# Hybrid decoder trunk on one core: the order of the first loads, and the place of the step that lays the tokens' norm factors along rows

## The chip, the cores and the metric

The kernel runs on one core of one Trainium2 chip. The metric is device time in microseconds (us) of one execution, as the median of several. The engines are named as in the profile: PE (matrix multiplies), PEld (its weight loads), DVE, ACT, POOL, and SP, whose only work here is to issue DMAs. Times inside the program are us from the start of the profiled span.

## The reference, cut to what matters

Two layers over 512 tokens of width 1024, in float32. Each layer normalizes the tokens, projects them with one large matrix, runs two kinds of attention over eight and four heads, gates, projects back and adds; then it adds a gated embedding.

```python
def rmsnorm(x, g, eps=RMS_EPS):
    xf = x.astype(jnp.float32)
    y = xf * lax.rsqrt(jnp.mean(xf * xf, axis=-1, keepdims=True) + eps)
    return (y * g.astype(jnp.float32)).astype(x.dtype)
...
    u = rmsnorm(h, norm_gain) @ w_in
    qa, ka, va, ga, qd, kd, vd, gd = jnp.split(u, list(np.cumsum(IN_SPLITS)[:-1]), axis=-1)
...
    y = jnp.concatenate([oa * jax.nn.silu(ga), od * jax.nn.silu(gd)], axis=-1) @ w_out
    h = h + y
    gate = jax.nn.sigmoid(rmsnorm(h, ple_norm_gain) @ w_ple_gate)
    return h + (p_i @ w_ple) * gate
```

Of `rmsnorm` the gain `g` belongs to a channel and the factor `rsqrt(mean(x*x)+eps)` to a token. The kernel uses that: it multiplies the gain into `x` ahead of the matmul and the token's factor into the result behind it.

## The kernel before, in words

**Precision and units.** A float32 operand is held as a high part and a low part (`hi`, `lo`), both in a rounded type; a product is three matmuls, high by high, high by low and low by high (`PASSES`, L317). A *unit* is one 128 x 512 result over 1024 channels: 8 blocks of 128 channels by 3, 24 matmuls with 512 columns. A *chunk* is four units, with a weight of 1024 x 512 that comes in four *pairs* (two blocks of channels, 512 KB each).

**Loads.** Every weight pair is loaded by SP into a staging tile (`stg`; three of them, and part of `of` as a fourth for the first chunk). ACT copies it into the ring (`ring`, five slots) as the high part, and DVE or POOL subtract to get the low part. The first layer's input comes twice: `xt`, the transpose (channels in rows), in four pieces of 512 KB, from which ACT makes the high parts (`xt_hi`: `xy<-fr,gt`, scaled by the gain) and DVE the low parts (`xt_lo`); and `x` by tokens, in four pieces of 512 KB, of which only the sums of squares are wanted (`x_sumsq` on ACT and DVE, then `rstd`: a tiny DVE step and a power on POOL for each of four groups of tokens, `st<-st`). `gt` holds the gains of the norms, 128 rows of 128 bytes. The first four pairs and `xt` pieces are needed together: pair r with piece r.

**The first chunk** (`vd`, `units_by_rows`, L482) goes by pairs, not by results: for pair r it does 6 matmuls into each of four results (banks `b_79` to `b_82`), 24 in all, and then takes pair r+1. Ahead of it PE runs `NWARM` matmuls on a tile of zeros (`warm_up`, `b<-pt`), which need no load.

**spread** (L527). The projections of q and k come out with tokens along columns, so the factors are needed along rows. `spread` lets PE transpose the four columns of factors, each broadcast to 128 columns (`b<-idt,st`, four small matmuls); ACT copies the result (`cr<-b`), and DVE multiplies it into the two tables of rotation (`cr<-ct,b`). Its first use is the rotation of the first q of the second chunk; the gates use it later. Its call for the first layer is L647, with a place of 2.5, in units of the plan (a chunk spans 4).

**What sets the order.** Nothing is written out in the order in which it runs. `Plan` gives each step a place; `Machine.schedule` (L189) takes all recorded instructions, gives each a wanted time (`want`: matmuls are laid end to end from `START`, everything else is counted back from its users, for a DMA by the lag in `lag`), and then plays the program against a table of costs: at each step it takes the engine that is free first and, of the instructions ready on it, the one with the earliest wanted time. The result is a fixed order on each engine. On the chip every engine takes its instructions in that order, so one that waits holds all behind it. SP's DMAs go through one queue; the model charges them at 230 bytes per ns (L272).

```python
            if e == "SP":
                t = max([t] + landed[-8:-7])
                free[e] = t + busy[i]
                dma = max(dma, t + 1.4) + done[i][1] / 230e3
```

The numbers of the cost model (L237, L272, `START`), `NWARM` and the place of `spread` are what the change touches.

Of the kernel before, what the change touches and what calls it, by code (L numbers as in the profile page):

```python
# [57 lines left out]
class Plan:  # L58
# [7 lines left out]
    def pe(self, t, us, f, *a):  # L66
        self.pieces.append((t, len(self.pieces), us, f, a))

    def at(self, t, us, f, *a):
        self.items.append((t, us, f, a))  # L70
# [16 lines left out]
class Machine:  # L87
# [101 lines left out]
    def schedule(self):  # L189
# [13 lines left out]
        busy, done = [0.0] * N, [None] * N  # L203
# [25 lines left out]

        clock, want = START, [None] * N  # L230
        for i in range(N):
# [4 lines left out]

        def lag(i):  # L237
            c = done[i]
            return c[0] + 2.0 + c[1] / 200e3 if isinstance(c, tuple) else c
        for i in range(N - 1, -1, -1):  # L240
            w = want[i] if want[i] is not None else end
            for s in succ[i]:
                w = min(w, want[s] - lag(i) - (MARGIN if eng[s] == "PE" and eng[i] != "PE" else 0.0))
            want[i] = w
# [4 lines left out]
        dma, landed = 0.0, []  # L249
# [5 lines left out]
        for _ in range(N):  # L255
            best = None
            for e, lst in waiting.items():
                if not lst:
                    continue
                t = max(free[e], min(ready_at[i] for i in lst))  # L260
                if best is None or t < best[0]:
                    best = (t, e)
            t, e = best
            i = min((i for i in waiting[e] if ready_at[i] <= t + 1e-9), key=lambda i: (want[i], i))
            waiting[e].remove(i)
            order.append((t, len(order), i))
            free[e] = t + busy[i]
            if e == "SP":

                t = max([t] + landed[-8:-7])  # L270
                free[e] = t + busy[i]
                dma = max(dma, t + 1.4) + done[i][1] / 230e3  # L272
                fin = dma + 0.6
                landed.append(fin)
            else:
                fin = t + done[i]
            for s in succ[i]:
                if eng[s] == "PE":

                    r = t + busy[i] if e == "PE" else fin + MARGIN  # L280
                else:
                    r = fin
                ready_at[s] = max(ready_at[s], r)
                left[s] -= 1
                if not left[s]:
                    waiting[eng[s]].append(s)
# [17 lines left out]

START = 8.0

MARGIN = 1.5

# [11 lines left out]
def trunk(tc, x, p, w_in, w_out, w_gate, w_ple, final_gain, tables, xt, gt, lams, sub, out):  # L322
# [7 lines left out]
    with tc.tile_pool(name="sb", bufs=1) as sb, tc.tile_pool(name="ps", bufs=1, space=PSUM) as psp, \  # L330
# [26 lines left out]
        RS0 = ST[:, 136:140]  # L357
# [38 lines left out]
        plan = Plan()  # L396
        at, pe = plan.at, plan.pe
        nbank = [0]
        NWARM = 14

        def bank():
            nbank[0] += 1
            return BANK[2 + (nbank[0] - 1) % 6]
# [123 lines left out]
        def spread(tt, rs, rot):  # L527
            b = {}

            def tr():  # L530
                b[0] = bank()
                for t in range(T):
                    PE.transpose(b[0][:, t * 128:(t + 1) * 128], rs[:, t:t + 1].to_broadcast([128, 128]), IDT)

            def f():
                ACT.activation(RB, b[0], AF.Copy)
                if rot:
                    DVE.tensor_mul(C0, C, b[0])
                    DVE.tensor_mul(SN0, SN, b[0])
            pe(tt, 0.436, tr)  # L540
            at(tt, 0.1, f)
# [57 lines left out]
        def warm_up():  # L599
            b = bank()  # L600
            for i in range(NWARM):
                mm(b, PT[:, 0, 0:128], PT[:, 0, 0:512], start=(i == 0), stop=(i == NWARM - 1))

# [23 lines left out]
        def st(us, f, *a):  # L627
            at(-10, 60 + us, f, *a)
# [13 lines left out]
        for t in range(T):  # L642
# [1 line left out]
            for h in range(2):  # L644
                st(3.1 + 0.3 * t, x_sumsq, t, h)
            st(3.2 + 0.3 * t, rstd, t, RS0)
        spread(2.5, RS0, True)  # L647


        nP = [0]  # L650
# [536 lines left out]
```

## Time and profile before

| what | value |
|---|---|
| median of three runs | 688.07 us (687.35 to 689.34) |
| profiled execution: its time | 687.14 us |
| profiled execution: its span | 685.1 us |
| PE busy | 672.7 us, 98% of the span |
| DVE, ACT, POOL busy | 435.1, 373.5, 383.4 us |
| chain that ended last | PE 94%, DVE 3%, DMA 1% |
| the DMAs from 12 to 24 us | some 410 GB/s |

The span runs from the first instruction to the last; 2.0 us of the profiled time lie outside it. A PE that is busy for 98% of the span leaves some 12 us in which it is not, and the timeline of PE shows where these are.

### The profile page before, as it was taken

How to read it: one execution, taken by the hardware profiler on the slowest of the kernel's cores; microseconds unless marked ns; L12 is line 12 of the kernel's file. 1: busy time of each engine (PE TensorE's matmuls, PEld its weight loads, DVE VectorE, ACT ScalarE, POOL GpSimd, SP SyncE). 2: the span in 40 equal slices, each digit the busy share in tenths (PEclk: the TensorE clock that was granted, in tenths of full speed). 3: DMA queues.
4: the chain of work that ended last, by engine and by line, in shares of the span. 5: the costliest groups of instructions: out<-in, count | busy, mean ns of one | idle time of the engine just before them, and what ended most of it. 6: DMA issues, size and time to landing. Idle time of an engine off the chain costs nothing.

```text
span 685.1 us, 9574 instructions
## 1 busy us (share of the span) xinstructions
PE 672.7 (98%) x3310; PEld 563.7 (82%) x3310; DVE 435.1 (64%) x839; ACT 373.5 (55%) x782; POOL 383.4 (56%) x290
## 2 busy tenths in 40 slices
PE   8999999999999999999999999999999999999995
PEld 6788888888888888888888888888888888788884
DVE  5447996657766884446443689874777678534334
ACT  6525756548888545524433457664787865353321
POOL 4669470876713357937484767266753245496311
PEclk9999999999999999999999999999999999999998
DMA  8656441444442532334152463333535262243002
GB/s 334 235 153 178 102 140 45 135 113 128 121 122 93 184 123 93 131 117 144 59 174 84 123 171 122 78 99 88 154 93 154 85 224 92 94 152 122 1 32 93
DMA packets 30961, 85.32 MB, mean 125 GB/s; under 512 B 4544, under 2 KB 4544, under 8 KB 30912
## 3 DMA queue, kind: packets, MB, share of 16 engines
q1 hardware_dynamic: 30912, 84.71, 39.9%
q8 instruction: 26, 0.43, 0.2%
q14 instruction: 23, 0.19, 0.1%
HBM read 63.72 MB, written 4.19 MB: 99 GB/s over the span
## 4 chain that ended last, share of the span: by engine, by line
PE 94%; DVE 3%; DMA 1%; issue 0%; ACT 0%; POOL 0%; SPq 0%; POOLq 0%; DVEq 0%; ACTq 0%
PE b L293 94%; DVE fr L293 2%; DMA gt<-in_gt_dram 1%; DVE misc L293 1%; DVE xy L293 0%; DVE ring L293 0%; POOL st L293 0%; ACT xy L293 0%; DVE of L293 0%; SPq L293 0%; DVE st L293 0%; POOLq L1183 0%; ACT of L293 0%; ACT misc L293 0%; DVEq L1183 0%
## 5 line engine op out<-in xcount | busy, mean ns | idle before, releaser
L293 PE MATMUL b<-xy,ring 128*128 128x512 f32 x1728 | 419.0, 393 | 0.2
L293 PEld LDWEIGHTS b<-xy,ring 128*128 128x128 f32 x1728 | 318.6, 188 | 63.6 <-DVE fr L293 1.9
L293 POOL TENSOR_TENSOR ring<-stg,ring 128x512 fp32r<-128x512 f32 x164 | 233.6, 1448 | 163.1 <-ACT ring L293 132.3
L293 PE MATMUL b<-ring,xy 128*128 128x512 f32 (+1 forms) x600 | 141.6, 385 | 2.6 <-ACT xy L293 2.4
L293 ACT ACTIVATE ring<-stg 128x1024 fp32r<-128x1024 f32 x95 | 99.9, 1057 | 51.4 <-PE b L293 33.5
L293 PEld LDWEIGHTS b<-ring,xy 128*128 128x128 f32 x600 | 107.4, 188 | 24.6 <-ACT xy L293 3.1
L293 ACT ACTIVATE fr<-fr,st 128x512 f32<-128x512 f32 (+3 forms) x193 | 101.7, 556 | 36.8 <-DVE st L293 34.2
L293 POOL TENSOR_TENSOR fr<-fr 128x512 f32<-128x512 f32 x53 | 74.0, 1399 | 30.1 <-ACT fr L293 25.6
L293 POOL TENSOR_TENSOR fr<-fr,cr 128x512 f32<-128x512 f32 x32 | 43.3, 1352 | 63.4 <-DVE fr L293 63.4
L293 DVE CUSTOM_DVE_ANT_0 fr<-b,ct 128x512 f32<-128x512 f32 (+3 forms) x128 | 58.5, 485 | 31.5 <-PE b L293 30.4
L293 DVE SCALAR_TENSOR_TENSOR xy<-fr,gt,xy 128x512 fp32r<-128x512 f32 x32 | 36.3, 1145 | 31.8 <-ACT xy L293 31.8
L293 PE MATMUL b<-qk 128*128 128x128 f32 (+3 forms) x256 | 52.4, 324 | 0.0
L293 DVE TENSOR_TENSOR ring<-stg,ring 128x512 fp32r<-128x512 f32 x26 | 34.7, 1334 | 21.7 <-ACT ring L293 21.7
L293 DVE TENSOR_TENSOR pt<-b,pt 128x384 fp32r<-128x384 f32 (+1 forms) x72 | 40.2, 592 | 12.0 <-ACT pt L293 11.6
L293 ACT ACTIVATE pt<-b 128x384 fp32r<-128x384 f32 (+1 forms) x72 | 34.6, 525 | 18.3 <-PE b L293 18.1
L293 PEld LDWEIGHTS b<-qk 128*128 128x128 f32 x256 | 39.0, 189 | 4.2 <-issue 0.3
L293 PEld LDWEIGHTS b<-idt,fr 128*128 128x128 f32 x284 | 34.0, 140 | 7.2 <-DVE fr L293 0.8
L293 ACT ACTIVATE nt<-fr 128x512 fp32r<-128x512 f32 x32 | 19.8, 624 | 36.7 <-POOL fr L293 36.7
L293 PE MATMUL b<-idt,fr 128*128 128x128 f32 x284 | 39.7, 272 | 0.0
L293 DVE TENSOR_TENSOR fr<-b,cr 128x512 f32<-128x512 f32 x48 | 32.6, 680 | 10.5 <-PE b L293 10.3
L293 POOL TENSOR_TENSOR st<-st 128x4 f32<-128x4 f32 (+1 forms) x20 | 18.0, 899 | 33.0 <-DVE st L293 32.4
L293 ACT ACTIVATE fr<-fr 128x512 f32<-128x512 f32 x26 | 16.4, 631 | 34.6 <-DVE fr L293 34.1
(78 smaller groups left out, 581.9 us busy)
## 6 DMA issues: line engine op xcount, KB each, us to landing
stg<-in_w_in_dram SPq DMA_DIRECT2D x63, 512.0 KB, 3.4
qk<-nt SPq DMA_DIRECT2D x128, 128.0 KB, 2.3
stg<-in_w_out_dram SPq DMA_DIRECT2D x16, 512.0 KB, 4.4
stg<-in_w_ple_gate_dram SPq DMA_DIRECT2D x16, 512.0 KB, 3.3
fr<-in_xt_dram SPq DMA_DIRECT2D x8, 512.0 KB, 5.3
stg<-in_w_ple_dram SPq DMA_DIRECT2D x4, 512.0 KB, 3.3
hsave<-fr SPq DMA_DIRECT2D x8, 256.0 KB, 2.0
fr<-hsave SPq DMA_DIRECT2D x4, 512.0 KB, 3.7
```

The lines of the kernel that those rows point to most:

```text
L293: getattr(self.eng[e], op)(*args, **kw)
```

## The change

In the cost model, a DMA of at most 64 KB is to be issued 4 us earlier than before with respect to its users, DMAs are charged at 300 instead of 230 bytes per ns, and the matmuls are laid out from 6.0 instead of 8.0 us. The warm-up has 10 matmuls instead of 14, and the first layer's `spread` has the place 3.3 instead of 2.5 (the first chunk spans 0 to 4). What is computed is the same.

```diff
         def lag(i):
             c = done[i]
-            return c[0] + 2.0 + c[1] / 200e3 if isinstance(c, tuple) else c
+            if isinstance(c, tuple):
+
+                return c[0] + (2.0 if c[1] > 65536 else 6.0) + c[1] / 200e3
+            return c
...
                 t = max([t] + landed[-8:-7])
                 free[e] = t + busy[i]
-                dma = max(dma, t + 1.4) + done[i][1] / 230e3
+                dma = max(dma, t + 1.4) + done[i][1] / 300e3
...
-START = 8.0
+START = 6.0
...
-        NWARM = 14
+        NWARM = 10
...
             for h in range(2):
                 st(3.1 + 0.3 * t, x_sumsq, t, h)
             st(3.2 + 0.3 * t, rstd, t, RS0)
-        spread(2.5, RS0, True)
+        spread(3.3, RS0, True)
```

Rows of the order below are one instruction each, or as many like it in a row as the `x` at the end says; the first word is a line of the kernel, and the changed kernel's lines are three further on (L296 for L293).

On SP, from the first DMA on, before:

```order
L293 DMA stg<-in_w_in_dram 128x1024
L293 DMA fr<-in_xt_dram 128x1024
L293 DMA gt<-in_gt_dram 128x32
L293 DMA stg<-in_w_in_dram 128x1024
L293 DMA fr<-in_xt_dram 128x1024
L293 DMA stg<-in_w_in_dram 128x1024
L293 DMA fr<-in_xt_dram 128x1024
L293 DMA fr<-in_x_dram 128x1024 x2
L293 DMA of<-in_x_dram 128x1024 x2
L293 DMA of<-in_w_in_dram 128x1024
L293 DMA fr<-in_xt_dram 128x1024
L293 DMA stg<-in_w_in_dram 128x1024 x3
```

And in the changed kernel:

```order
L296 DMA gt<-in_gt_dram 128x32
L296 DMA stg<-in_w_in_dram 128x1024
L296 DMA fr<-in_xt_dram 128x1024
L296 DMA stg<-in_w_in_dram 128x1024
L296 DMA fr<-in_xt_dram 128x1024
L296 DMA stg<-in_w_in_dram 128x1024
L296 DMA fr<-in_xt_dram 128x1024
L296 DMA of<-in_w_in_dram 128x1024
L296 DMA fr<-in_xt_dram 128x1024
L296 DMA fr<-in_x_dram 128x1024 x2
L296 DMA of<-in_x_dram 128x1024
L296 DMA stg<-in_w_in_dram 128x1024
```

The gains come first instead of third, the fourth weight pair and `xt` piece stand ahead of all of `x`, and the last piece of `x` now follows the first weight pair of the second chunk.

On ACT, in the first chunk, from the third `xt` piece to the end of the fourth, before (`cr<-b` is the copy of `spread`, `fr,st<-fr` and `of,st<-of` are sums of squares):

```order
L293 ACTIVATE xy_63<-fr,gt 128x512 x2
L293 ACTIVATE fr,st<-fr 128x512 x2
L293 ACTIVATE of,st<-of 128x512 x2
L293 ACTIVATE ring<-of 128x1024
L293 ACTIVATE cr<-b_86 128x512
L293 ACTIVATE xy_63<-fr,gt 128x512 x2
L293 ACTIVATE ring<-stg 128x1024 x2
```

And now, as far as the copy of `spread` (`xy_64<-b_79` to `xy_64<-b_81` write out results of the first chunk):

```order
L296 ACTIVATE xy_63<-fr,gt 128x512 x2
L296 ACTIVATE ring<-of 128x1024
L296 ACTIVATE xy_63<-fr,gt 128x512 x2
L296 ACTIVATE fr,st<-fr 128x512 x2
L296 ACTIVATE of,st<-of 128x512
L296 ACTIVATE ring<-stg 128x1024
L296 ACTIVATE of,st<-of 128x512
L296 ACTIVATE ring<-stg 128x1024
L296 ACTIVATE xy_64<-b_79,st 128x4x128
L296 ACTIVATE xy_64<-b_80,st 128x4x128
L296 ACTIVATE ring<-stg 128x1024
L296 ACTIVATE xy_64<-b_81,st 128x4x128
```

The high parts of the fourth `xt` piece stood behind `cr<-b`; now `cr<-b` comes only after three results are written out. On PE the four transposes of `spread` move in the same way, from ahead of the 24 matmuls of the fourth pair to behind the 18th of them.

Nor is the rest of the program in the same order. On PE 705 rows become 712, and in the attention parts of both layers groups of matmuls trade places. The first such place with transposes of attention weights (`b<-idt,fr`), before:

```order
L293 MATMUL b_79<-xy_63,ring 128x512 x9
L293 MATMUL b_86<-idt,fr 128x128 x3
L293 MATMUL b_81<-qk 128x128 x2
L293 MATMUL b_81<-qk 128x256 x2
L293 MATMUL b_82<-qk 128x384 x2
L293 MATMUL b_83<-qk 128x512 x2
L293 MATMUL b_84<-idt,fr 128x128 x4
L293 MATMUL b_85<-idt,fr 128x128 x3
L293 MATMUL b_79<-xy_63,ring 128x512 x6
```

And now:

```order
L296 MATMUL b_79<-xy_63,ring 128x512 x3
L296 MATMUL b_81<-qk 128x128 x2
L296 MATMUL b_81<-qk 128x256 x2
L296 MATMUL b_82<-qk 128x384 x2
L296 MATMUL b_83<-qk 128x512 x2
L296 MATMUL b_79<-xy_63,ring 128x512 x3
L296 MATMUL b_84<-idt,fr 128x128 x4
L296 MATMUL b_85<-idt,fr 128x128 x3
L296 MATMUL b_79<-xy_63,ring 128x512 x3
L296 MATMUL b_86<-idt,fr 128x128 x3
```

Here the scores `b<-qk` moved ahead by six matmuls of the projection and one group of transposes went to the end. The tail of the program, from the last chunk's last result on, is unchanged.

## Rows read from the trace of the kernel before

**Rows 1.** The page: busy time, share and count of each engine.

```profile
PE 672.7 (98%) x3310; PEld 563.7 (82%) x3310; DVE 435.1 (64%) x839; ACT 373.5 (55%) x782; POOL 383.4 (56%) x290
```

**Rows 2.** PE's waits, whole span, longest in total: us, times, longest.

```profile
PE b L293 <- ACT xy L293: 2.4, 2, 1.3
```

**Rows 3.** Timeline of PE, 0 to 60 us: start, length, what, [idle before <-releaser].

```profile
1.44 5.38 PE L293 MATMUL b<-pt 128*128 128x512 f32 x14 [1.44 <-DVE st L293]
7.94 16.98 PE L293 MATMUL b<-ring,xy 128*128 128x512 f32 x72 [1.11 <-ACT xy L293]
24.76 0.60 PE L293 MATMUL b<-idt,st 128*128 128x128 f32 x4
26.65 6.08 PE L293 MATMUL b<-ring,xy 128*128 128x512 f32 x24 [1.30 <-ACT xy L293]
32.57 20.90 PE L293 MATMUL b<-xy,ring 128*128 128x512 f32 x90
```

**Rows 4.** Chain that ended last, in order of time: its first long run on PE.

```profile
8.72 16.65 PE b L293 x74
```

**Rows 5.** Timeline of ACT in the first chunk.

```profile
4.15 1.06 ACT L293 ACTIVATE ring<-stg 128x1024 fp32r<-128x1024 f32 x1 [1.92 <-DMA stg<-in_w_in_dram]
7.17 1.34 ACT L293 ACTIVATE xy<-fr,gt 128x512 fp32r<-128x512 f32 x2 [1.96 <-DMA gt<-in_gt_dram]
...
17.62 0.63 ACT L293 ACTIVATE of<-of 128x512 f32<-128x512 f32 x1 [0.56 <-DMA of<-in_x_dram]
...
25.39 0.60 ACT L293 ACTIVATE cr<-b 128x512 f32<-128x512 f32 x1 [5.43 <-PE b L293]
25.89 1.32 ACT L293 ACTIVATE xy<-fr,gt 128x512 fp32r<-128x512 f32 x2
```

**Rows 6.** Timeline of SP: start and length of the issue of a DMA.

```profile
0.73 0.39 SPq L293 DMA_DIRECT2D stg<-in_w_in_dram  x1
1.17 0.42 SPq L293 DMA_DIRECT2D fr<-in_xt_dram  x1
1.64 0.42 SPq L293 DMA_DIRECT2D gt<-in_gt_dram  x1
...
9.93 0.33 SPq L293 DMA_DIRECT2D fr<-in_xt_dram  x1
```

**Rows 7.** DMAs issued in 1.1:1.6, 1.6:2.0 and 9.5:10.3; last column: us to landing.

```profile
fr<-in_xt_dram SPq DMA_DIRECT2D x1, 512.0 KB, 5.5
...
gt<-in_gt_dram SPq DMA_DIRECT2D x1, 16.0 KB, 5.4
...
fr<-in_xt_dram SPq DMA_DIRECT2D x1, 512.0 KB, 10.2
```

**Rows 8.** Stretches: length, busy (x) by engine, granted clock, DMA share, GB/s.

```profile
4.40:5.40 1.00, 1.00 (x3) 0.77 (x3) 0.16 (x1) 0.81 (x1) 0.05 (x1) 1.00 1.00 160
5.40:6.40 1.00, 1.00 (x5) 0.81 (x4) 0.53 (x1) 0.00 (x0) 1.00 (x1) 1.00 0.64 208
16.00:20.00 4.00, 4.00 (x19) 3.30 (x18) 2.90 (x13) 2.50 (x5) 3.33 (x4) 1.00 1.03 409
```

**Rows 9.** Timeline of POOL, 18 to 42 us.

```profile
17.54 2.41 POOL L293 TENSOR_TENSOR st<-st 128x1 f32<-128x1 f32 x3
...
28.24 7.75 POOL L293 TENSOR_TENSOR ring<-stg,ring 128x512 fp32r<-128x512 f32 x6 [6.41 <-PE b L293]
```

**Rows 10.** Stretches: the warm-up's first ten, and the span's end; columns as above.

```profile
1.44:5.56 4.12, 4.12 (x10) 3.29 (x11) 0.32 (x1) 1.83 (x3) 2.19 (x5) 1.00 0.90 262
...
677.40:685.10 7.70, 0.00 (x0) 0.00 (x0) 2.16 (x7) 1.02 (x2) 1.42 (x3) 0.76 0.19 70
```

**Rows 11.** Timelines of DVE and PE at the first transposes of attention weights.

```profile
66.84 3.91 DVE L293 SCALAR_TENSOR_TENSOR fr<-fr,st 128x512 f32<-128x512 f32 x4
...
71.81 0.93 PE L293 MATMUL b<-idt,fr 128*128 128x128 f32 x7
72.49 1.64 PE L293 MATMUL b<-xy,ring 128*128 128x512 f32 x6
```

## The prediction

> **What bounds the kernel now.** I read the page first: PE is busy for 672.7 of 685.1 us, 98% [rows 1], and no other engine comes near. So what moves the end is PE's work, or the 12.4 us in which PE stands still. The timeline of PE says where these lie [rows 3]: 1.44 us ahead of the first instruction, 1.11 us ahead of the first real matmul, 1.30 us ahead of the last 24 of the first chunk, and 7.70 us behind the last matmul [rows 10]. That is 11.55; less than 1 us is left for all the rest, so from 27 us to 677 us PE runs through. The list of PE's waits agrees: its largest entry is 2.4 us in two waits, both for the high parts of the input, `xy` [rows 2]. These two, both in the first chunk, are all that a change of the first loads can win, unless it shortens the work itself, and it does not: the same matmuls are done, less four of the warm-up. A gain there is kept, though, since PE is the bound from there to the end, and every later load waits for a place that PE frees.
>
> **Term 1: spread leaves the way of the fourth pair.** Its four transposes stand ahead of the last 24 matmuls and start at 24.76; the second chunk starts at 32.57 [rows 3]. So 24 matmuls and four transposes take 7.81 us. What should they take? The third to the 72nd matmul, 70 of them, run from 8.72 [rows 4] to 24.76: 0.229 us each. Seven transposes of the same size take 72.49 - 71.81 = 0.68 us, 0.097 each [rows 11]. 24 x 0.229 + 4 x 0.097 = 5.89, so 1.92 us are lost. Why: ACT copies the transposes' result at 25.39, having stood 5.43 us with its next instruction waiting for PE, and only then makes the high parts of the fourth `xt` piece, at 25.89 [rows 5]. That piece was issued at 9.93 [rows 6] and took 10.2 us [rows 7]: it had landed at 20.1. The wait is one of order alone. In the new order ACT makes these high parts ahead of the sums of squares and of `spread`'s copy, and the piece itself lands earlier (below, some 14 us). I take the whole 1.92. The transposes now stand behind the 18th of the 24, and need all four factors. **What is late next** there: the last piece of `x` moves back from place 11 to 14 of the queue. 512 KB take 1.28 us at 409 GB/s [rows 8]. With the first `xt` at 6.5 (term 2) the fourth lands six transfers later, at 14.2, the last of `x` five after that, at 20.6. Now it lands at 17.6 [rows 5] and the last power on POOL ends at 17.54 + 2.41 = 19.95 [rows 9], 2.35 later; the new order puts two low parts of weights ahead of that power, 2 x 1.29 (7.75 / 6) [rows 9]. So the factors are there between 23.0 and 25.6, and PE, with the last 24 from 24.16 on (term 2), asks for them at 24.16 + 18 x 0.229 = 28.3. Cover: 2.7 us or more; beyond it each us late costs one.
>
> **Term 2: the gains come first.** The first real matmul waits for ACT, and ACT for `gt` [rows 5]. `gt` was issued third, at 1.64, and took 5.4 us: landed at 7.07, while the first `xt` piece landed at 1.17 + 5.5 = 6.67 [rows 6, 7] and the first weights at some 4.15 [rows 5]. With `gt` first (at 0.73), weights and `xt` are issued 0.44 and 0.47 later, and `xt` is the one that is late. When? *Early end:* weights at 4.15 + 0.44, `xt` one transfer of 1.28 behind them: 5.87, a gain of 1.2. *Late end:* all that slows `xt` today stays (6.67 + 0.47), and `gt` costs the 0.40 by which it now lands behind `xt`: 7.54, a loss of 0.47. What decides is a dip: from 4.4 to 6.4 us the queue moved 160 and 208 GB/s, where 409 is normal [rows 8]. That is 2 x (1 - 184 / 409) = 1.1 us, just where `gt`'s 128 rows of 128 bytes pass. I take the dip to be theirs. In front it comes before the weights, but 0.44 of it falls into the time until these are issued; 0.66 is left. `xt` then lands at 5.87 + 0.66 = 6.5, a gain of 0.6 (from -0.5 to 1.2); PE's run of 70 shifts by it, and the last 24 start at 24.76 - 0.6 = 24.16.
>
> A rule speaks against this part: the Trainium skill, DMA: Bandwidth & Descriptors, Specifications, has it that pieces under 512 B are not moved at line rate, and its table under Bandwidth gives 0.68 us for 4 KB and 0.95 for 64 KB. By it `gt` in front would cost an estimated 0.8 us instead of my 1.1, and the gain would be 0.9. The dip agrees in kind; no row shows `gt` alone.
>
> **The rest of the change.** Four warm-up matmuls fewer: nothing. PE ended them at 6.82 and then waited 1.11 us [rows 3]; now they end near 5.9 and it waits longer, unless the clock falls (rival 2). Pairs 1 and 2: the 72 matmuls of the first three pairs run without another wait [rows 3], and their loads keep their order. The second chunk's weights: before, POOL made their low parts from 28.24 on, behind ACT's stop [rows 9]; now two pairs are done before the chunk starts, at 32.57 - 2.5 = 30.1. The third has its high part behind two results on ACT: the second of these is ready at 24.16 + 12 x 0.229 = 26.9, then 0.7 and 1.06 us of ACT [rows 5] and 2 x 1.29 of POOL: 31.3 to 31.6. PE wants it 12 matmuls into the chunk, at 32.9. Cover 1.3 us. The reordered attention parts: same work, bounded by no row; I put them at nothing, from -0.5 (the less than 1 us of PE idle there) to +0.7, three matmuls' time at one place.
>
> **Sum.** 1.92 + 0.6 = 2.5 us. The profiled execution, 687.14 us (span 685.1 and 2.0 outside it), would become 684.6; it lies 0.9 below the median of 688.07, and from the median I get **685.6**. 0.3%, about what a measurement of this kernel can tell from no change, is 2.06 us: below 686.0 is faster, above 690.1 slower.
>
> **Rivals.**
> 1. *The start gains nothing.* If the dip is not `gt`'s, or `xt` stays as late as it is, term 2 is between 0 and -0.5, and 1.4 to 1.9 us remain: 686.2 to 686.7, within 0.3%. A late third pair in the second chunk would look alike. For it: no row shows `gt` without a queue ahead of it. Against it: the dip stands in `gt`'s place.
> 2. *The clock.* The first ten warm-up matmuls take some 4.1 us [rows 10], 0.41 each: 512 columns at 1.2 GHz take 0.427. The last ones of the 14 and all that follow step at 0.23, the level of 2.4 GHz, though the column of the granted clock prints 1.00 throughout. So the clock rose as about the tenth ran, and now there are ten, with 1.4 us of nothing behind them. If it does not rise, or falls again, each real matmul costs 0.2 more. Held for as many matmuls as at the start (ten), that is 2.0 us: a gain of 0.5, 687.6. It would take 13 to eat the gain. For it: ten is just enough and no more. Against it: up to the rise PE does the very same as before.
> 3. *Slower: the attention parts.* PE's order there was changed at many places in both layers. At the first, DVE ends the weights at 66.84 + 3.91 = 70.75, and PE transposes them at 71.81 [rows 11]: 1.06 us of slack, and the change takes the transposes ahead by three matmuls and three transposes, 1.0 us. Where such a group comes too early, PE stops for what is lacking, up to the three matmuls' 0.69 us. Four such places eat the gain; from seven on (4.8 us) the kernel is slower by over 0.3%: 690.4. Against it: the steps feeding these places were moved with them, and PE now waits nowhere there.
> 4. *More:* the new order closes the little idle time that is left, and `gt` costs nothing: 3.2 to 3.7 us, 684.4 to 684.9.
>
> **How the numbers follow.** Forecast (gain 1.9 to 3.2) 0.60; rival 1 0.16; rival 2 0.13; rival 3 0.07, of it 0.05 above 690.1; rival 4 0.04. Of the forecast's 0.60 about 0.48 lie below 686.0 after the spread of a median; with rival 4 and a remainder of rival 1, faster is 0.55. Slower 0.06, the rest, 0.39, within 0.3%. The range leaves out rival 3, half of rival 2 and the end of rival 4: 684.3 to 687.6. It takes in both ends of term 2 (685.0 and 686.7).
>
> **What would show it.** Right: `gt` lands first, ACT's first `xy` near 6.6 waits for `xt`; the first 96 matmuls of the chunk run without a hole, the four transposes among the last; the second chunk starts near 30.1; PE's waits no longer hold the 1.3 us on `xy`; the end is as much earlier as the second chunk's start. Term 2 is wrong if that first `xy` is not before 7.17; term 1 if PE stops ahead of the transposes or at 20 to 25 us. Rival 2 shows as real matmuls that step at 0.43; rival 3 as new PE waits after 45 us, with the second chunk on time and the end not.

## The result, and the profile after

The changed kernel is slower: 691.42 us (690.46 to 692.54) against 687.21 for the kernel before beside it, a ratio of 1.0062 [1.005, 1.0073], where 685.6 us and a gain were forecast. The profiled execution took 691.7 us, with a span of 689.8; that is 4.7 us more span than before.

The page after, first the busy times; it answers to [rows 1].

```profile
PE 674.5 (98%) x3306; PEld 564.6 (82%) x3306; DVE 437.6 (63%) x839; ACT 373.0 (54%) x782; POOL 383.9 (56%) x290
```

PE has four matmuls fewer and is busy 1.8 us longer. So part of the loss is in the matmuls themselves, and the rest in waits. The list of PE's waits after, us in total, times, longest; it answers to [rows 2]:

```profile
PE b L296 <- ACT xy L296: 3.4, 2, 2.2
PE b L296 <- DVE st L296: 1.4, 1, 1.4
PE b L296 <- DMA qk<-nt: 1.4, 3, 0.7
PE b L296 <- DVE ring L296: 0.6, 1, 0.6
```

The second line is the start of the program and was there before. The third and fourth are new, and the first holds one wait that is new. Where they lie, and where the first chunk stands, is seen in PE's timeline after (start, length, what, idle before it), which answers to [rows 3]; `b<-qk` are scores of attention, `qk<-nt` the moves inside the chip that bring normalized k and q to the scores:

```profile
1.45 4.64 PE L296 MATMUL b<-pt 128*128 128x512 f32 x10 [1.45 <-DVE st L296]
8.33 23.32 PE L296 MATMUL b<-ring,xy 128*128 128x512 f32 x90 [2.25 <-ACT xy L296]
31.49 0.60 PE L296 MATMUL b<-idt,st 128*128 128x128 f32 x4
31.84 1.64 PE L296 MATMUL b<-ring,xy 128*128 128x512 f32 x6
...
70.42 1.51 PE L296 MATMUL b<-qk 128*128 128x128 f32 x8 [0.70 <-DMA qk<-nt]
...
106.98 1.51 PE L296 MATMUL b<-qk 128*128 128x128 f32 x8 [0.26 <-DMA qk<-nt]
...
253.32 7.04 PE L296 MATMUL b<-xy,ring 128*128 128x512 f32 x28 [0.60 <-DVE ring L296]
...
439.72 1.52 PE L296 MATMUL b<-qk 128*128 128x128 f32 x8 [0.45 <-DMA qk<-nt]
...
578.14 3.19 PE L296 MATMUL b<-xy,ring 128*128 128x512 f32 x13 [1.11 <-ACT xy L296]
...
677.13 4.47 PE L296 MATMUL b<-ring,xy 128*128 128x256 f32 x36
```

The hole of [rows 3] ahead of the last 24 matmuls of the first chunk is gone, as forecast. Yet the chunk is no shorter. How far after is behind before, at the same matmul of the projections (starts read from the two timelines of PE):

| matmul | before | after | behind |
|---|---|---|---|
| first real one | 7.94 | 8.33 | 0.39 |
| first of the second chunk | 32.57 | 33.31 | 0.74 |
| first of the third | 55.95 | 56.37 | 0.42 |
| first of the fourth | 86.47 | 88.14 | 1.67 |
| 865th (tenth chunk) | 265.06 | 267.23 | 2.17 |
| 1537th | 452.35 | 455.24 | 2.89 |
| 1921st | 573.89 | 578.14 | 4.25 |
| the last 36 | 672.71 | 677.13 | 4.42 |

So two things happened. The first chunk gave back what it won, and behind the second chunk's start another 3.7 us were lost. From there to the last 36 matmuls PE is busy for 640.38 of 643.82 us, where it was 639.59 of 640.14 before. So it stands still for 3.4 us instead of 0.55, and 3.1 of these are the five stops that the timeline shows; the other 0.8 of the 3.7 are in matmuls that count as busy for longer.

What ate the first chunk's gain is the clock. Two stretches of after (length; busy and number of instructions for PE, PEld, DVE, ACT, POOL; granted clock, DMA share, GB/s):

```profile
8.33:13.95 5.62, 5.62 (x13) 4.36 (x14) 5.13 (x6) 5.20 (x7) 3.17 (x2) 1.00 1.03 419
13.95:31.49 17.54, 17.54 (x79) 14.40 (x77) 9.51 (x20) 9.19 (x17) 8.95 (x10) 1.00 0.90 347
```

and the first 13 real matmuls of before:

```profile
7.94:11.35 3.41, 3.35 (x13) 2.43 (x14) 2.74 (x4) 2.95 (x5) 1.79 (x1) 1.00 1.02 413
```

Thirteen matmuls took 5.6 us where they took 3.4, at 0.43 us each, which is 512 columns at 1.2 GHz; from 13.95 on they step at 0.23. That is 2.2 us, and term 1's gain was 1.9. The printed clock is 1.00 in all three rows, but in the first of them it tells nothing: the trace of after has no record of the granted clock ahead of 13.96 us, and the column prints 1.00 where there is none. There the number of matmuls in a stretch tells the level. In after none of the ten warm-up matmuls ran at the higher level either; they step at 0.43.

The start itself, in ACT's timeline after, which answers to the first rows of [rows 5]:

```profile
5.04 1.06 ACT L296 ACTIVATE ring<-stg 128x1024 fp32r<-128x1024 f32 x1 [2.81 <-DMA stg<-in_w_in_dram]
7.56 1.33 ACT L296 ACTIVATE xy<-fr,gt 128x512 fp32r<-128x512 f32 x2 [1.47 <-DMA fr<-in_xt_dram]
```

The first weights are there 0.89 us later and the first high parts 0.39 later than before. ACT waits for `xt` now, not for `gt`, as forecast; but `xt` is late.

### The profile page after: what moved, and what is told of

It is laid out like the page before. It is cut to its first block, busy times and chain, and to the rows that moved or that the text cites. A ratio compares the mean times of both kernels' runs of the same rounds, so it can differ in the third digit from the quotient of the medians.

```text
span 689.8 us, 9560 instructions
## 1 busy us (share of the span) xinstructions
PE 674.5 (98%) x3306; PEld 564.6 (82%) x3306; DVE 437.6 (63%) x839; ACT 373.0 (54%) x782; POOL 383.9 (56%) x290
## 4 chain that ended last, share of the span: by engine, by line
PE 86%; DVE 7%; DMA 2%; issue 2%; ACT 2%; POOL 0%; SPq 0%; POOLq 0%; DVEq 0%; ACTq 0%
PE b L296 86%; DVE fr L296 3%; DVE misc L296 1%; DMA qk<-nt 1%; DMA fr<-in_xt_dram 1%; DVE of L296 1%; ACT fr L296 1%; DVE xy L296 1%; DVE nt L296 0%; DVE pt L296 0%; POOL st L296 0%; ACT xy L296 0%; ACT misc L296 0%; DVE st L296 0%; ACT pt L296 0%
## 5 line engine op out<-in xcount | busy, mean ns | idle before, releaser
L296 PE MATMUL b<-xy,ring 128*128 128x512 f32 x1728 | 419.8, 393 | 1.9 <-ACT xy L296 1.1
L296 PEld LDWEIGHTS b<-xy,ring 128*128 128x128 f32 x1728 | 318.1, 188 | 65.9 <-DVE fr L296 1.7
L296 POOL TENSOR_TENSOR ring<-stg,ring 128x512 fp32r<-128x512 f32 x164 | 234.3, 1453 | 161.8 <-ACT ring L296 156.8
L296 PE MATMUL b<-ring,xy 128*128 128x512 f32 (+1 forms) x600 | 144.2, 390 | 2.2 <-ACT xy L296 2.2
L296 ACT ACTIVATE ring<-stg 128x1024 fp32r<-128x1024 f32 x95 | 99.8, 1057 | 55.8 <-PE b L296 30.0
L296 PEld LDWEIGHTS b<-ring,xy 128*128 128x128 f32 x600 | 109.2, 191 | 24.0 <-ACT xy L296 3.0
L296 ACT ACTIVATE fr<-fr,st 128x128 f32<-128x128 f32 (+3 forms) x193 | 101.9, 556 | 35.9 <-DVE st L296 33.2
L296 POOL TENSOR_TENSOR fr<-fr 128x512 f32<-128x512 f32 x53 | 74.5, 1408 | 34.7 <-ACT fr L296 30.6
L296 POOL TENSOR_TENSOR fr<-fr,cr 128x512 f32<-128x512 f32 x32 | 44.4, 1387 | 64.0 <-DVE fr L296 64.0
L296 DVE CUSTOM_DVE_ANT_0 fr<-b,ct 128x384 f32<-128x384 f32 (+3 forms) x128 | 58.0, 485 | 28.8 <-PE b L296 28.1
L296 DVE SCALAR_TENSOR_TENSOR xy<-fr,gt,xy 128x512 fp32r<-128x512 f32 x32 | 37.4, 1178 | 28.7 <-ACT xy L296 28.7
L296 PE MATMUL b<-qk 128*128 128x128 f32 (+3 forms) x256 | 52.3, 323 | 1.4 <-DMA qk<-nt 1.4
L296 DVE TENSOR_TENSOR pt<-b,pt 128x384 fp32r<-128x384 f32 (+1 forms) x72 | 40.3, 593 | 15.7 <-ACT pt L296 15.5
L296 DVE TENSOR_TENSOR ring<-stg,ring 128x512 fp32r<-128x512 f32 x26 | 32.6, 1253 | 24.8 <-ACT ring L296 24.8
L296 ACT ACTIVATE pt<-b 128x384 fp32r<-128x384 f32 (+1 forms) x72 | 34.6, 524 | 22.6 <-PE b L296 21.3
L296 PEld LDWEIGHTS b<-qk 128*128 128x128 f32 x256 | 39.2, 189 | 6.5 <-issue 1.5
L296 ACT ACTIVATE nt<-fr 128x512 fp32r<-128x512 f32 x32 | 20.0, 624 | 40.5 <-POOL fr L296 40.5
L296 PEld LDWEIGHTS b<-idt,fr 128*128 128x128 f32 x284 | 34.1, 140 | 6.6
L296 PE MATMUL b<-idt,fr 128*128 128x128 f32 x284 | 39.3, 272 | 0.0
L296 DVE TENSOR_TENSOR qk<-fr,nt 64x512 fp32r<-64x512 f32 x32 | 28.8, 901 | 11.9 <-ACT nt L296 11.4
L296 DVE TENSOR_TENSOR fr<-b,cr 128x512 f32<-128x512 f32 x48 | 32.6, 678 | 4.7 <-PE b L296 4.5
L296 POOL TENSOR_TENSOR st<-st 128x4 f32<-128x4 f32 (+1 forms) x20 | 17.3, 867 | 32.7 <-DVE st L296 32.0
```

The lines of the kernel that those rows point to most:

```text
L296: getattr(self.eng[e], op)(*args, **kw)
```

## The experiments

Three causes had to be told apart: the clock behind a shorter warm-up; the gains in front; and the order behind the first chunk, which is another because the model charges DMAs at another rate. The expectations call the clock theory A and the order theory B; theory C is that B comes from the charge of one kind of DMA. The late `spread` is the fourth part and the one meant to win. Of the new waits only `qk<-nt` has a DMA in it: its moves of 128 KB are issued by SP one behind the other, and SP's timeline after shows the distance, 3.68 us for six, 0.61 each, and they land as far apart, 0.62 on the mean:

```profile
64.21 3.68 SPq L296 DMA_DIRECT2D qk<-nt  x6
```

That is about 215 bytes per ns. A model that charges 300 believes such a move to be done sooner than it is. A row of 512 KB loads does reach more (419 GB/s above), so one figure cannot be right for both.

All times below are medians, beside runs of the kernel before on the same chip. Where a wanted time of PE would have changed with the number of warm-up matmuls, `START` was set so that the order of all else stays as it was.

**Ten warm-up matmuls in the kernel before.**

```diff
-START = 8.0
+START = 8.9067
...
-        NWARM = 14
+        NWARM = 10
```

> The kernel before with 10 warm-up matmuls in place of 14; START is moved by the four matmuls' modelled time, so that every other instruction keeps its place. Theory A (the clock): in the trace of the changed kernel the first 14 or so real matmuls step at 0.427 us until 14.0 us; ten warm-ups end too early to get the high level, so here the first real matmuls run at 0.427 as well: 13 to 20 of them, 0.2 us each, the second chunk starts at 35 to 36 instead of 32.6, and the time is 2 to 3 us more, 689 to 690. Rival (the loss has nothing to do with the warm-up, the level is chance of the run): the second chunk starts at 32.6 in the profiled run or the time agrees with before within 0.7 us.

Measured: 687.79 us (686.15 to 689.97, 12 runs) against 686.45, ratio 1.0019 [1.0009, 1.003]: 1.3 us more, where 2 to 3 were expected. The profiled run is one of the longest, 689.86. Its PE timeline:

```profile
1.45 4.63 PE L293 MATMUL b<-pt 128*128 128x512 f32 x10 [1.45 <-DVE st L293]
9.02 18.80 PE L293 MATMUL b<-ring,xy 128*128 128x512 f32 x72 [2.94 <-ACT xy L293]
```

and the stretch from its first real matmul on:

```profile
9.02:13.69 4.67, 4.67 (x11) 3.62 (x12) 4.18 (x6) 4.23 (x6) 2.23 (x2) 1.00 1.02 418
```

Eleven matmuls at 0.42 each, which is the lower level, with nothing else of the change. The twelve times lie in three groups, three near 686.2, six from 687.6 to 688.4, three near 689.9; the first group has the time of before. So the price is not paid in every execution, and the level is in part the chance of the run, as the rival has it. The run with the old rate, below, shows the same: its warm-up has ten as well, and in its profiled execution, the shortest of its eleven, the first real matmuls step as at the higher level. In this profiled one `gt` landed 6.5 us after its issue, where [rows 7] has 5.4, which made the start late as well.

**The late spread alone.**

```diff
-        spread(2.5, RS0, True)
+        spread(3.3, RS0, True)
```

> The kernel before with the place of spread alone changed, 3.3 for 2.5; this also puts the loads of x behind the fourth pair. 14 warm-ups, gt third on the queue, the model's rate 230. Theory: term 1 of the prediction is right and hidden in the changed kernel by other losses: the hole ahead of the last 24 matmuls is gone, the second chunk starts at 30.6 to 30.8 instead of 32.57, and the time is 1.9 us less than before, 685.1 to 685.6. Rival (putting x last starves something later, and that is the changed kernel's loss): the second chunk is on time but later stages are not, and the time is no better than before.

Measured: 685.27 (684.72 to 686.08, 11 runs) against 686.45, ratio 0.9981 [0.9973, 0.999]: a gain of 1.2 us, not of 1.9. PE's timeline:

```profile
7.47 22.40 PE L293 MATMUL b<-ring,xy 128*128 128x512 f32 x96 [1.05 <-ACT xy L293]
29.71 2.88 PE L293 MATMUL b<-xy,ring 128*128 128x512 f32 x12
32.43 0.60 PE L293 MATMUL b<-idt,st 128*128 128x128 f32 x4
```

With the rate left at 230 the transposes of `spread` fall into the second chunk, 12 matmuls in. The first chunk has no hole at all and the second starts 2.86 us earlier, 0.47 of it because the first real matmul of this run is earlier. But the second chunk then takes 24.6 us instead of 23.4. The four transposes are 0.4 of that; most of the rest are longer steps at 35.6, 39.5 and 41.6 us, 0.3 each. At the first two the weight load waits for POOL's `ring`, at the third the wait is put down to DVE. The cover of 1.3 us that the prediction gave these weights is used up here.

**The model's rate alone.**

```diff
-                dma = max(dma, t + 1.4) + done[i][1] / 230e3
+                dma = max(dma, t + 1.4) + done[i][1] / 300e3
```

> The kernel before with the rate of DMAs in the model alone changed, 300 for 230. It moves nothing ahead of the fourth pair of the first chunk but some 99 places of PE's order behind it. Theory B (the order of the attention parts): in the changed kernel PE waits for the moves of q and k (at 70, 107 and 439 us), and once each at 253 and 578 us; the profile loses 3.7 us between the second chunk's start and the end. So here the first chunk is as before, within 0.5 us, PE waits for qk<-nt in the same places, and the time is 3 to 4 us more, 690 to 691. Rival (all comes from the first chunk): within 1 us of before, 686.5 to 688.

Measured: 687.18 (686.41 to 689.49, 11 runs) against 686.45, ratio 1.0012 [1.0003, 1.0021]. The expectation, that the first chunk would stay as it was, missed: the rate also moved the transposes, which now stand behind the 60th matmul of the first chunk instead of the 72nd, where the stop does not arise. So the time is the one that the rival gave, but not by its reason.

PE's timeline:

```profile
21.39 0.60 PE L293 MATMUL b<-idt,st 128*128 128x128 f32 x4
21.74 8.43 PE L293 MATMUL b<-ring,xy 128*128 128x512 f32 x36
30.02 16.26 PE L293 MATMUL b<-xy,ring 128*128 128x512 f32 x71
...
673.10 4.47 PE L293 MATMUL b<-ring,xy 128*128 128x256 f32 x36
```

The second chunk starts 2.55 earlier than before (32.57), and yet the last 36 matmuls start 0.39 later (672.71): 2.9 us are lost behind the first chunk, by this one constant. PE's waits show the same two kinds as after:

```profile
PE b L293 <- DMA qk<-nt: 0.9, 2, 0.6
PE b L293 <- DVE ring L293: 0.6, 1, 0.6
```

**The gains first, alone.**

```diff
-            return c[0] + 2.0 + c[1] / 200e3 if isinstance(c, tuple) else c
+            if isinstance(c, tuple):
+                return c[0] + (2.0 if c[1] > 65536 else 6.0) + c[1] / 200e3
+            return c
```

> The kernel before with the lag of small DMAs alone changed: gt is issued first on the queue instead of third, nothing else moves. My prediction gave this 0.6 us of gain (from -0.5 to 1.2); the changed kernel's trace has its first real matmul at 8.33 instead of 7.94. Theory: gt in front delays the first weights and xt by more than it saves, the first real matmul comes at 8.2 to 8.5, and the time is 0.2 to 0.5 us more, 687.4 to 687.7. Rival (the late start belongs to the fewer warm-ups or to the order of the other loads): the first real matmul comes at 7.0 to 7.5 and the time is 0.4 to 0.9 us less.

Measured: 687.18 (686.83 to 687.84, 11 runs) against 686.45, ratio 1.001 [1.0002, 1.0019]: a loss of 0.7 us, a little over the 0.2 to 0.5 expected. ACT's first high parts start at 7.37, 0.20 later than in [rows 5], and wait for `xt`. The two stretches of the dip in [rows 8], in this run:

```profile
4.40:5.40 1.00, 1.00 (x5) 0.79 (x5) 0.00 (x0) 0.95 (x1) 0.00 (x0) 1.00 0.83 184
5.40:6.40 1.00, 0.87 (x4) 0.38 (x2) 0.69 (x1) 0.11 (x1) 0.75 (x1) 1.00 0.89 221
```

`gt` is long gone by then, it landed 1.7 us after its issue at 0.73; the dip is still there. It is not `gt`'s.

**The change with 14 warm-up matmuls.** Edits here and in the next two are against the changed kernel.

```diff
-START = 6.0
+START = 5.0933
...
-        NWARM = 10
+        NWARM = 14
```

> The changed kernel with 14 warm-up matmuls for 10, START moved by their modelled time so that nothing else moves. Theory A (the clock costs the changed kernel up to 2.7 us, by chance of the run): the first real matmuls step at 0.23 us from the start, the runs lie within 1.5 us of each other, and the time is 1.3 to 2.7 us less than the changed kernel's, that is 2 to 3 us (0.3 to 0.4%) over before. Rival (the low level comes from the order of the loads, not from the warm-up): as the changed kernel, 4 us over before.

Measured: 689.48 (689.02 to 689.71, 5 runs) against 686.71, ratio 1.0039 [1.0026, 1.0051]. From 1.0062 that is 1.6 us given back. PE's timeline:

```profile
1.45 5.37 PE L295 MATMUL b<-pt 128*128 128x512 f32 x14 [1.45 <-DVE st L295]
8.06 21.05 PE L295 MATMUL b<-ring,xy 128*128 128x512 f32 x90 [1.24 <-ACT xy L295]
...
30.78 15.57 PE L295 MATMUL b<-xy,ring 128*128 128x512 f32 x68
...
674.99 4.47 PE L295 MATMUL b<-ring,xy 128*128 128x256 f32 x36
```

and, of its waits, those that are new:

```profile
PE b L295 <- DMA qk<-nt: 1.6, 3, 0.9
PE b L295 <- DVE ring L295: 0.7, 1, 0.7
```

The first chunk now takes 30.78 - 8.06 = 22.72 us; it took 32.57 - 7.94 = 24.63. The whole of term 1 is there, 1.91. And behind it everything is lost again: the second chunk starts 1.79 earlier than before, the last matmuls 2.28 later.

**The change with the old rate.**

```diff
-                dma = max(dma, t + 1.4) + done[i][1] / 300e3
+                dma = max(dma, t + 1.4) + done[i][1] / 230e3
```

> The changed kernel with the model's rate of DMAs back at 230; 10 warm-ups, gt first, spread late. Theory B (the order behind the first chunk costs 3.7 us): from the second chunk's start to the last matmul it takes as long as before, within 0.3 us, without a wait of PE for qk<-nt; the time is 3 to 4 us less than the changed kernel's, within 1 us of before. Rival (the stalls come from the first chunk's new order, START or the few warm-ups): PE still waits for qk<-nt and the time stays 3 us or more over before.

Measured: 687.03 (685.78 to 688.06, 11 runs) against 686.71, ratio 1.0006 [0.9997, 1.0015]. PE waits only at its start and ahead of the first real matmul; the other waits are gone. One part of the expectation missed: from the second chunk's start to the last 36 matmuls it should have taken as long as before, and takes 1.2 us longer. The old rate also puts `spread` into the second chunk, and the third piece of `x` behind that chunk's first weights; the second chunk alone is 1.3 us longer. Nor does this run say which of the DMAs charged at 300 do the harm.

**The change with the old rate for the small moves only.** Loads of 512 KB stay at 300, so the first chunk's order is that of the change.

```diff
-                dma = max(dma, t + 1.4) + done[i][1] / 300e3
+                dma = max(dma, t + 1.4) + done[i][1] / (300e3 if done[i][1] > 140000 else 230e3)
```

> The changed kernel with the model's rate at 230 for DMAs of up to 128 KB alone (the moves of q and k); weights and x stay at 300. In the traces SP issues one such move each 0.61 us (six in 3.67), which is what 128 KB take at 215; 300 lets the model have them each 0.45. Theory C (scores are placed too early because these moves are charged too little): PE's waits for qk<-nt go, 1.5 to 2 us of the 3.7 behind the first chunk with them. Whether the stops at 253 and 578 us go too, it leaves open; if they do, all 3.7. Rival (the rate of the weights makes the bad order): the waits for qk<-nt stay, and the time is within 1 us of the changed kernel's.

Measured: 686.82 (686.23 to 687.95, 11 runs) against 686.71, ratio 1.0005 [0.9996, 1.0014]: 3.9 us of the loss given back by the charge of the 128 KB moves. The list of PE's waits is now

```profile
PE b L296 <- ACT xy L296: 2.2, 1, 2.2
PE b L296 <- DVE st L296: 1.4, 1, 1.4
```

and the stops at 70, 107, 253, 440 and 578 us are not there. Its timeline again shows the clock's part:

```profile
8.08 22.59 PE L296 MATMUL b<-ring,xy 128*128 128x512 f32 x90 [2.25 <-ACT xy L296]
```

and the stretch of 4 us behind the start of its real matmuls:

```profile
8.40:12.40 4.00, 3.95 (x11) 2.82 (x10) 3.16 (x5) 3.45 (x5) 1.79 (x1) 0.57 1.02 419
```

Eleven matmuls in 4 us; the same stretch holds 18 where the clock is up (the run with everything mended, below), and this time the column says so, 0.57: here the records begin at 5.39, and from 8.81 to 12.22 they have the lower level.

**The late spread, with the gains second.** Against the kernel before. The first weights are not held up then.

```diff
-            return c[0] + 2.0 + c[1] / 200e3 if isinstance(c, tuple) else c
+            if isinstance(c, tuple):
+                return c[0] + (2.0 if c[1] > 65536 else 5.0) + c[1] / 200e3
+            return c
...
-        spread(2.5, RS0, True)
+        spread(3.3, RS0, True)
```

> The kernel before with the place of spread at 3.3 and gt second on the queue, between the first weights and the first xt piece; 14 warm-ups, rate 230. Theory: with gt behind the weights it delays only xt, by 0.2 to 0.4 us, while third it lands 0.05 to 1.7 us after xt: so the first real matmul comes at 7.2 to 7.7 and the time is 0 to 0.5 us less than with spread moved alone, 0.2 to 0.3% under before. Rival (what gt delays costs as much wherever it stands ahead of xt): as with gt first, 0.5 us over spread alone, 0.1% under before.

Measured: 689.87 (688.84 to 690.3, 5 runs) against 686.71, ratio 1.0043 [1.003, 1.0055]; a miss, since the late spread alone won 1.2 us. The first `xt` piece took 7.6 us from issue to landing, by its row of the DMAs:

```profile
fr<-in_xt_dram SPq DMA_DIRECT2D x1, 512.0 KB, 7.6
```

and PE started late, as its timeline shows, and ran seven of its first nine real matmuls at 0.43 although 14 warm-up matmuls had gone ahead:

```profile
10.05 23.85 PE L295 MATMUL b<-ring,xy 128*128 128x512 f32 x96 [2.51 <-ACT xy L295]
```

Why so small a transfer in second place costs 2 us is not settled.

**The moves' charge alone.** Against the kernel before: only DMAs of up to 128 KB are charged at 300.

```diff
-                dma = max(dma, t + 1.4) + done[i][1] / 230e3
+                dma = max(dma, t + 1.4) + done[i][1] / (230e3 if done[i][1] > 140000 else 300e3)
```

> The kernel before with the moves of q and k alone charged at 300 in the model, weights and x at 230: the other half of the change of rate. Theory C (too low a charge for these moves is what spoils the order behind the first chunk): PE waits for qk<-nt, the way from the second chunk's start to the last matmul is 2 to 4 us longer than before, and the time is 2 to 4 us more. Rival (only the two rates together, or an accident of the order, do it): within 1 us of before.

Measured: 689.12 (689.0 to 689.22, 5 runs) against 686.49, ratio 1.0034 [1.0021, 1.0046]. Nothing of the first chunk is changed by intent, and the kernel loses 2.6 us, all of it behind the second chunk's start: that one is 0.69 us earlier than before (the first real matmul is 0.67 earlier), the last 36 matmuls are 1.79 later. But the stops in PE's timeline are not those that were expected:

```profile
246.44 13.92 PE L293 MATMUL b<-xy,ring 128*128 128x512 f32 x57 [1.03 <-DVE fr L293]
575.39 9.79 PE L293 MATMUL b<-xy,ring 128*128 128x512 f32 x41 [1.10 <-DVE fr L293]
```

The list of PE's waits has no `qk<-nt` in this run; PE stops for DVE, in these two places. The size came as theory C has it, and its reason did not: here the moves' charge sets the loss, and not because the moves themselves come late at PE. Each charge gives another order, and the orders for 300 have their own places where PE asks too early. All runs together say the same. From the third chunk's first matmul to the last 36, behind all that happens to `spread`, the nine kernels that charge the moves at 230 take 616.4 to 617.4 us in their profiles, and the four that charge them at 300 (after, this one, the rate alone, and the change with 14 warm-up matmuls) 619.2 to 621.2. Only these two charges were run, so it is not shown that 230 is better because it is nearer to 215.

**What is good of the change, without the rest.** Against the kernel before: the late spread, 512 KB loads at 300, smaller DMAs at 230, 14 warm-up matmuls, the gains third as they were.

```diff
-                dma = max(dma, t + 1.4) + done[i][1] / 230e3
+                dma = max(dma, t + 1.4) + done[i][1] / (300e3 if done[i][1] > 140000 else 230e3)
...
-START = 8.0
+START = 5.0933
...
-        spread(2.5, RS0, True)
+        spread(3.3, RS0, True)
```

> The changed kernel with its three losses undone: moves of q and k charged at 230 (weights and x stay at 300), 14 warm-ups, gt third again; spread stays late (START moved by the modelled time of the warm-ups). Theory (the three are all that is wrong, term 1 is right): the second chunk starts at 29.7 to 30.6, its weights are there, no wait of PE for qk<-nt, and the time is 1.9 to 2.6 us under before, 684.0 to 684.8 beside a before of 686.6; it beats spread alone (1.2 us under before). Rival (the second chunk's weights eat a part, as they do with spread alone, where it takes 24.6 us for 23.4): 0.8 to 1.4 us under before.

Measured: 684.59 (684.41 to 685.22, 6 runs) against 686.49, ratio 0.9969 [0.9957, 0.9981]. It is faster than both kernels. PE's timeline:

```profile
7.91 21.04 PE L293 MATMUL b<-ring,xy 128*128 128x512 f32 x90 [1.41 <-ACT xy L293]
28.78 0.60 PE L293 MATMUL b<-idt,st 128*128 128x128 f32 x4
29.13 1.63 PE L293 MATMUL b<-ring,xy 128*128 128x512 f32 x6
30.61 15.58 PE L293 MATMUL b<-xy,ring 128*128 128x512 f32 x68
...
671.04 4.47 PE L293 MATMUL b<-ring,xy 128*128 128x256 f32 x36
```

and the same 4 us, with the clock up:

```profile
8.40:12.40 4.00, 3.94 (x18) 3.05 (x17) 3.48 (x5) 3.55 (x6) 2.03 (x2) 1.00 1.03 420
```

The first real matmul stands where it stood before (7.91, 7.94), the second chunk starts 1.96 earlier and the last matmuls 1.67: of the gain in the first chunk nearly all reaches the end.

**The same with the gains first.** The edit of the gains-first run on top of this one; it is the changed kernel with 14 warm-up matmuls and the old charge for the small moves.

> The same as e9_mended, with gt first on the queue; nothing else differs. Price of gt in front by itself: my prediction gave 0.6 us of gain; the kernel before with gt first alone was 0.7 us (0.1 to 1.3) slower. Theory: the first real matmul comes 0.1 to 0.7 us later and the time is 0.2 to 0.8 us over that of e9_mended. Rival: 0.3 to 0.9 us under it.

Measured: 685.09 (684.84 to 685.56, 10 runs) against 686.49, ratio 0.9978 [0.9969, 0.9987]. It is 0.5 us behind the one with the gains third, and the two intervals overlap; with the 0.7 us of the gains-first run, and ACT waiting for `xt` in both, I take the gains in front to cost some 0.6 us. A gain shows in neither. The landings in the traces agree: the later of `gt` and the first `xt` piece lands at 7.09 to 7.47 in the six profiled runs with the gains first, and at 6.41 to 7.08 in five of the six with them third (8.16 in the sixth, the one with ten warm-up matmuls).

## Why the prediction was wrong, step by step

**The account.** Each part was taken out of the changed kernel or done alone. In us, from the medians and ratios above: late `spread`, with the 512 KB loads charged at 300, -1.9; ten warm-up matmuls, +1.6; gains in front, +0.6; the small moves charged at 300, +3.9. The sum is +4.2, and 0.0062 x 687 is 4.3. Each part is known to about 1 us by its interval, so that they meet this closely is luck; their order of size is not. Taking out the second and the fourth together gives 0.9978 where the single runs add up to 0.9982, so no sign is seen that these two parts touch each other.

**What bounds the kernel** was read rightly: PE. What I drew from it, that only its two waits can be won, is true for a gain. It says nothing of a loss: a PE that ran through 650 us without a stop of any size did so in one order, and this order was changed.

**Term 1 was right.** 1.92 us forecast; the first chunk is 1.91 shorter in the change with 14 warm-up matmuls and 1.93 in the mended kernel, whose second chunk starts at 30.61 where near 30.1 was forecast. The factors for the transposes were there in time: in no run does PE stop ahead of the transposes where they stand among the last matmuls of the chunk. The cover of the second chunk's weights was rightly called thin; with the late `spread` alone, where the transposes fall into the second chunk, it is overdrawn.

**Term 2 failed at "I take the dip to be theirs".** With `gt` in front and landed 1.7 us after issue, 184 and 221 GB/s remain at 4.4 to 6.4 us in place of 160 and 208. That is the condition of rival 1. So nothing was to be had by moving `gt` away from there, and its price in front is paid by what stands behind it: the first weights are 0.89 us later in the profiled run of after, 0.45 of it SP's issue, and the first `xt` piece, forecast to land at 6.5, lands at 7.47. That is near the term's late end. The sign was wrong, -0.6 forecast against some +0.6. The range of the term, from a gain of 1.2 to a loss of 0.5, all but held it. The price that the prediction took from the Trainium skill, DMA: Bandwidth & Descriptors, Bandwidth, by which the gain was 0.9, would have been further off; that table is for DMAs that GpSimd issues, and these are SP's.

**"Four warm-up matmuls fewer: nothing" failed.** It was rival 2, put at 0.13, and its mechanism came: "if it does not rise, or falls again". In the profiled runs with ten, none of the ten ran at 0.23. PE then did nothing from the end of the last to the first real matmul. In the changed kernel it found the low level there, and 13 matmuls cost 2.2 us, where I had priced ten at 2.0. The medians give 1.6 and 1.3 us, less, since not each execution pays. What I set against it, that up to the rise PE does the same as before, was wrong as an argument. The rise in [rows 3] comes with the tenth matmul in one execution; in other traces, with the same work of PE, it comes at 4.5 us or not by 7.1 (last section), so one row could not tell when it would come with ten. Of the four profiled runs with ten, the real matmuls begin at the lower level in two, fall to it with the third in one, and stay at the higher level in one.

**"The reordered attention parts: I put them at nothing" was the step that decided.** It was +3.9 us, and I bounded it at +0.7. The mechanism is rival 3's, a group of matmuls ahead of what feeds it, though not at the group that it names: the transposes of weights, which follow DVE, did not stop PE, the scores in front of them did, which follow the moves. At 69.72 PE asked for the scores, six matmuls and three transposes earlier in its order than before, and the moves were there 0.70 us later. Rival 3 gave 0.69 us to a place and asked for seven to reach 690.4. The timeline shows five stops of 0.26 to 1.11 us, at 70, 107, 253, 440 and 578 us, 3.1 together. The size of a place was about right. What failed was the sentence against it, that the steps feeding these places were moved with them, and with it the chance of 0.07. The moves that feed the scores were not moved ahead: SP issues the six of them at 64.21, where it was 63.83 before. And the constant could have been held against the trace of before, where SP takes 3.67 us for these six:

```profile
63.83 3.67 SPq L293 DMA_DIRECT2D qk<-nt  x6
```

The diff says 300 bytes per ns for every DMA, and a move of 128 KB goes at 215. A model with that rate may ask for scores too early.

The stops that are not `qk<-nt` need a word. At 578 PE waits for ACT's `xy<-of`, ACT for DVE, and DVE is slow there while POOL runs beside it (its row of low parts began at 572.13). DVE's instruction, and the one of ACT that PE waits for, in the timelines of after:

```profile
573.91 1.78 DVE L296 TENSOR_TENSOR xy<-of,xy 128x512 fp32r<-128x512 f32 x1
```

```profile
577.42 0.63 ACT L296 ACTIVATE xy<-of 128x512 fp32r<-128x512 f32 x1 [0.61 <-DVE of L296]
```

In before the like instruction ran ahead of POOL's row of low parts, which began at 569.16, and took 0.69 us:

```profile
567.64 0.69 DVE L293 TENSOR_TENSOR xy<-of,xy 128x512 fp32r<-128x512 f32 x1
```

Each of the two traces has 16 instructions of this kind: those clear of POOL, but for 0.03 of their time at most, take 0.67 to 0.69 us, those beside POOL 1.36 to 1.78. So a shift by a few us puts DVE's work beside POOL's and makes it up to 2.6 times as long. The two stops of the run with the moves' charge alone have the same in front of them: DVE's like instructions at 242.30 and 571.16 take 1.78 us there, beside POOL. That the stop at 578, and the one at 253, go when the moves' charge goes back was shown; by which of the many moved rows was not. Nor is it settled why the order made for the moves at 300, alone, brings only stops for DVE and none for moves.

**The range** left out rival 3 and so did not hold the time. Its top, 687.6, was made of the start's terms alone.

## What to carry to other kernels

Where a cost model makes the order, a constant that is changed for the sake of one stage orders the whole program anew; look through the order of every stage behind it for groups that moved ahead, and hold the constant against the trace for each kind of transfer (here 0.61 us for a 128 KB move, but 419 GB/s for a row of 512 KB loads). A warm-up has to be read as a row of steps, at 0.43 or 0.23 us, up to the first real matmul, with what PE does between. And a change of four parts that loses can hold one that wins: taken apart, this one gave 0.9969.

## What the runs showed of the hardware

- The step of the warm-up matmuls fell from 0.43 to 0.23 us at different times in kernels in which PE does the same up to there: at 4.5 us (gains first), 4.9 (what is good of the change), 5.7 (before), and not by 7.1 (rate alone, gains second). And the clock went back: in the run with the small moves at the old rate and in the one with the gains second, the first two real matmuls step as in runs at the higher level (0.34 and 0.45), and the next seven at 0.43. The real matmuls ran low at first behind waits of 2.25 (twice), 2.51 and 2.94 us, and high behind those of 1.96 us and less; these are single executions, and I make no rule of them.
- The dip of the DMA rate between 4.4 and 6.4 us is there wherever `gt` stands: 160 and 208 GB/s with it third, 152 and 197 second, 184 and 221 first, alone. In all thirteen traces these two stretches have 152 to 250 GB/s, where the one from 8.4 to 12.4 us has 396 to 423. What makes the dip is open.
- 16 KB in 128 rows of 128 bytes took 1.6 to 1.8 us from issue to landing in first place, 3.2 in second, and 4.8 to 6.5 in third. The Trainium skill, DMA: Bandwidth & Descriptors, Specifications, has it that pieces under 512 B are not moved at line rate. The trace of after agrees: a packet of 128 bytes took 12 ns on its DMA engine on the mean, some 11 bytes per ns, and one of 4096 bytes, in the first 12 us, 191 ns, some 21. The 128 packets were done within 0.4 us, so the rate of the small pieces is not what makes the 1.7 us. Why the second place costs the `xt` load behind it 2 us, no run here shows.
